# Row maximum over 67 MB: fewer, larger middle loads, more columns on GpSimd, and a first store in two halves

## The chip, the cores and the metric

The kernel runs on one core of one Trainium2 chip. The metric is device time in microseconds, the median of the runs. The profile is one more execution, taken by the hardware profiler; its span leaves out a little that the device time has (162.0 us of span beside 163.79 us for the same profiled run). "DVE" is VectorE, "PE" is TensorE, "ACT" is ScalarE, "POOL" is GpSimd, "SP" is SyncE, which here only issues loads. A trailing q (SPq, ACTq) means the engine's own queue of instructions, where DMA transfers are issued.

## The reference

The input is a float32 array of 32 x 512 x 1024. The output is the largest value of each row of 1024.

```python
def setup_inputs():
    batch, seq, dim = 32, 512, 1024
    return {"x": np.random.randn(batch, seq, dim).astype(np.float32)}

def reference(x: np.ndarray) -> np.ndarray:
    return np.max(x, axis=-1).astype(np.float32)
```

There are 16384 rows, 67.11 MB in all, and 64 KB of output. Laid over 128 partitions this is 128 rows for each partition. In this document a **block** is one row for each of the 128 partitions: 128 x 1024 values, 512 KB. There are 128 blocks to load and to reduce. A block has 1024 columns, which are 8 **column blocks** of 128.

## The kernel before

The kernel streams the blocks through a ring in SBUF that has room for 47 of them. The list `BLOCKS` says how many blocks each load carries. The loads are numbered from 0 in that order. The last two blocks come in four **pieces**, two for each, cut by column at the widths in `PIECES`.

```python
BLOCKS = [
    [2, 13, 13, 15, 14, 11, 11, 10, 8, 8, 7],
    [4, 3, 2, 2, 1, 1, 1],
]
RING = 47

SHARED = {10: (3, 6), 12: (2, 6), 14: (1, 6), 17: (1, 2)}

PIECES = [(604, 420), (568, 456)]

PLAN = """
    d0 d1 d2 d3 d4 d5 d6 d7 d8 d9 t0 d10 t1 t2 p10 d11 b0 b1 t3 d12 t4 p12 d13 b2 m10 t5 d14
    p14 d15 b3 b4 d16 m12 p17 t6 f0 b5 f1 f2 b6 m14 f3 m17
""".split()
```

`SHARED` names the loads in which GpSimd takes a part: `10: (3, 6)` means that of the last 3 blocks of load 10, six column blocks each go by another way. `PLAN` is the order of the work. Each engine takes its own steps in this order:

- `d` (direct): VectorE reduces the blocks of a load that are not shared, in one instruction.
- `t` (turn): TensorE transposes the shared column blocks into PSUM, ScalarE copies them to SBUF, GpSimd takes the maximum over the partitions.
- `b` (back): TensorE turns row 0 of GpSimd's result back into a column.
- `p` (partial): VectorE reduces the columns of a shared block that GpSimd does not take.
- `m` (merge): VectorE takes the maximum of the partial results.
- `f`: VectorE reduces a piece; the second piece of a row includes the result of the first, which lies one element ahead of it.

```python
def maximum(out, in_):
    return in_turn("DVE", nc.vector.reduce_max(out=out, in_=in_, axis=X))
# ...
def turn(k):
    j, r, q = chunks[k]
    m, parts = shared[j]
    W = q * parts * P
    ps = psum.tile([P, D], F32)
    # ... q * parts transposes on TensorE into ps
    sb = turned.tile([P, D], F32)
    in_turn("ACT", nc.scalar.copy(out=sb[:, :W], in_=ps[:, :W]))
    top = allr.tile([P, D], F32)
    in_turn("POOL", nc.gpsimd.partition_all_reduce(
        top[:, :W], sb[:, :W], P, bass_isa.ReduceOp.max))
```

A turn holds whole blocks, and at most `max(1, 8 // parts)` of them. A load is issued as soon as the steps that read its place in the ring are done (the wait is left to the semaphores); pieces follow after the last whole load.

```python
while issued < len(loads):
    start, n, src, _ = loads[issued]
    if any(readers[j] and s < start + n and start < s + k
           for j, (s, k, _, _) in enumerate(loads[:issued])):
        return
    load = nc.sync.dma_start(out=rows(issued), in_=src)
    issued += 1
# ...
while pieces:
    nc.sync.dma_start(out=pieces[0][0], in_=pieces[0][1])
    pieces.pop(0)
```

A load's place in the ring starts where the last one ended, or at 0 when it does not fit any more. Two stores end the kernel. The first carries the 112 blocks of the first list and is held until the first `f` is done, the second carries the last 16.

```python
for dst, src in views[:-1]:
    store = nc.scalar.dma_start(out=dst, in_=src)
    tc.add_manual_dep(store.ins, behind.ins.name, SYNC, reason="behind the loads")
nc.scalar.dma_start(out=views[-1][0], in_=views[-1][1])
```

Of the kernel before, what the change touches and what calls it, by code (L numbers as in the profile page):

```python
# [10 lines left out]


BLOCKS = [
    [2, 13, 13, 15, 14, 11, 11, 10, 8, 8, 7],
    [4, 3, 2, 2, 1, 1, 1],
]
RING = 47


SHARED = {10: (3, 6), 12: (2, 6), 14: (1, 6), 17: (1, 2)}  # L20

PIECES = [(604, 420), (568, 456)]

PLAN = """
    d0 d1 d2 d3 d4 d5 d6 d7 d8 d9 t0 d10 t1 t2 p10 d11 b0 b1 t3 d12 t4 p12 d13 b2 m10 t5 d14
    p14 d15 b3 b4 d16 m12 p17 t6 f0 b5 f1 f2 b6 m14 f3 m17  # L30
""".split()

NOSYNC = mybir.DependencyInfo(mybir.DependencyClass.NoSync, mybir.DependencyReason.DATA)
# [4 lines left out]
def kernel(  # L38
# [5 lines left out]
    nc = tc.nc  # L44
    P = 128
# [27 lines left out]
    def maximum(out, in_):  # L73
# [8 lines left out]
        out=colno, data0=ident, data1=ident, initial=-1.0, op0=ALU.add, op1=ALU.mult))  # L82
    in_turn("DVE", nc.vector.transpose(out=rowno, in_=colno[:, :32]))  # L83
    for q in range(1, P // 32):
        part = rowno[q * 32:(q + 1) * 32, 0:1]
        in_turn("DVE", nc.vector.tensor_scalar(  # L86
            out=part, in0=part, scalar1=float(q * 32), scalar2=None, op0=ALU.add))
    identity = in_turn("DVE", nc.vector.tensor_scalar(  # L88
        out=ident, in0=colno, scalar1=rowno[:, 0:1], scalar2=None, op0=ALU.is_equal))

    loads = []
    views = []
    last = len(PIECES)
    first = at = 0
    for sizes in BLOCKS:
        S = sum(sizes) + last * (sizes is BLOCKS[-1])
        xb = xf[first * P:(first + S) * P, :].rearrange("(p i) d -> p i d", p=P)
        dst = bass.AP(tensor=of.tensor, offset=of.offset + first * P, ap=[[S, P], [1, S]])
# [9 lines left out]
    assert first == I  # L108
    shared = [SHARED.get(j, (0, C)) for j in range(len(loads))]

# [68 lines left out]
    room = I + at * D  # L179
    for q in range(len(PIECES[0])):  # L180
        for r, widths in enumerate(PIECES):
            c, w = sum(widths[:q]), widths[q]
# [49 lines left out]
            if behind is None:  # L232
                behind = inst

    for dst, src in views[:-1]:
        store = nc.scalar.dma_start(out=dst, in_=src)
        tc.add_manual_dep(store.ins, behind.ins.name, SYNC, reason="behind the loads")
    nc.scalar.dma_start(out=views[-1][0], in_=views[-1][1])

# [28 lines left out]
```

## Time and profile before

| | |
|---|---|
| device time | 163.84 us, median of 3 runs (163.75 to 163.88) |
| span of the profiled run | 162.0 us |
| moved by the loads | 67.11 MB in 22 transfers (18 loads, 4 pieces) |
| VectorE busy | 135.5 us, 84% of the span |
| GpSimd busy | 16.2 us, of it 16.0 us in 7 reductions over the partitions |
| TensorE busy | 13.5 us; ScalarE 6.4 us |

The profile has the busy time of each engine, a picture of the span in 40 slices, the DMA queues, the chain of work that ended last, groups of instructions with busy time and the mean of one, and a timeline in order of time. A timeline row has the start, the length, the engine, the source line, the operation, what it writes and reads, the shape and how many instructions were merged into the row; the bracket at its end says how long the engine sat idle before it and what ended that. The queue numbered q1 carries the loads and q10 the stores.

### The profile page before, as it was taken

Reading aid. Unit: us, or ns where it says so; the run is one execution under the profiler, and the core shown is the slowest. Engines: PE = TensorE matmul, PEld = TensorE weight load, DVE = VectorE, ACT = ScalarE, POOL = GpSimd, SP = SyncE. Lnnn points to the kernel's source line nnn. Section 1 sums busy time; section 2 is a strip of 40 time slices with the busy share of each in tenths; the row PEclk is TensorE's granted clock in tenths of the full one; section 3 lists DMA queues with packets and bytes.
Section 4 is the critical chain, followed back from the end, with each engine's and each line's share of the span. In section 5 each row is a group of like instructions: output and inputs, shape, how many; then the busy total and the mean of one; then the engine's idle time right before and its main releaser. Section 6 shows DMA issues by size and latency. Waiting matters only on the chain.

```text
span 162.0 us, 306 instructions
## 1 busy us (share of the span) xinstructions
PE 13.5 (8%) x76; PEld 11.6 (7%) x76; DVE 135.5 (84%) x37; ACT 6.4 (4%) x8; POOL 16.2 (10%) x11
## 2 busy tenths in 40 slices
PE   0000000000000000000000000000000000746662
PEld 0000000000000000000000000000000000736541
DVE  3500079978996399989999999999999999999994
ACT  3000000000000000000000000000000000231220
POOL 0000000000000000000000000000000000197991
PEclk9999999999999999999999999999999999996555
DMA  5999999997999979999898999799999999999991
GB/s 172 508 421 421 421 421 421 473 550 303 485 485 485 396 311 425 453 405 534 356 534 356 489 400 465 344 485 388 421 485 388 424 418 453 409 431 415 407 390 37
DMA packets 3456, 67.18 MB, mean 415 GB/s; under 512 B 640, under 2 KB 896, under 8 KB 1536
## 3 DMA queue, kind: packets, MB, share of 16 engines
q1 hardware_dynamic: 3168, 67.11, 96.9%
q10 hardware_dynamic: 288, 0.07, 0.2%
HBM read 67.11 MB, written 0.07 MB: 415 GB/s over the span
## 4 chain that ended last, share of the span: by engine, by line
DVE 49%; DMA 46%; another core or an unknown queue 3%; SPq 1%; issue 0%; DVEq 0%
DVE ring L74 47%; DMA ring<-in_x_dram 46%; DVE got L74 1%; SPq L209 1%; DVEq L263 0%
## 5 line engine op out<-in xcount | busy, mean ns | idle before, releaser
L74 DVE TENSOR_REDUCE ring<-ring 128x1 f32<-128x1024 f32 (+12 forms) x21 | 131.5, 6293 | 23.3 <-DMA ring<-in_x_dram 23.1
L146 POOL PARTITION_ALL_REDUCE top<-sb x7 | 16.0, 2351 | 142.2 <-ACT sb L144 142.2
L138 PE MATMUL ps<-ident,ring 128*128 128x128 f32 x38 | 9.0, 424 | 141.3 <-DMA ring<-in_x_dram 141.0
L138 PEld LDWEIGHTS ps<-ident,ring 128*128 128x128 f32 x38 | 7.5, 224 | 141.5 <-issue 141.5
L144 ACT COPY sb<-ps 128x768 f32<-128x768 f32 (+1 forms) x7 | 5.2, 738 | 150.3 <-PE ps L138 148.9
L156 PE MATMUL got<-ident,top 1*128 1x1 f32 x38 | 4.6, 230 | 4.3 <-POOL top L146 2.9
L156 PEld LDWEIGHTS got<-ident,top 1*128 1x128 f32 x38 | 4.0, 188 | 6.0 <-POOL top L146 5.3
L74 DVE TENSOR_REDUCE got<-ring 128x3 f32<-128x768 f32 (+3 forms) x4 | 3.0, 753 | 0.0
L144 ACT ACT_TABLE_LOAD x1 | 1.3, 1283 | 0.7 <-PEq L252 0.7
L79 DVE MEMSET ident<- 128x128 f32 x1 | 0.2, 165 | 0.8 <-PEq L252 0.8
L74 DVE TENSOR_REDUCE ring<-got 128x3 f32<-128x21 f32 (+3 forms) x4 | 0.6, 160 | 0.0
L86 DVE TENSOR_SCALAR rowno<-rowno 32x1 f32<-32x1 f32 x3 | 0.4, 146 | 0.1
L81 DVE TENSOR_TENSOR_SCAN colno<-ident 128x128 f32<-128x128 f32 x1 | 0.4, 425 | 0.0
L88 DVE TENSOR_SCALAR ident<-colno,rowno 128x128 f32<-128x128 f32 x1 | 0.3, 286 | 0.0
L83 DVE STREAM_TRANSPOSE rowno<-colno 128x32 f32<-128x32 f32 x1 | 0.2, 211 | 0.0
L252 POOL MEMSET const-float32-0.0<- 128x1 f32 x1 | 0.1, 98 | 0.2 <-issue 0.2
L252 POOL MEMSET const-bfloat16-1.0<- 128x1 bf16 x1 | 0.1, 102 | 0.0
L252 POOL MEMSET const-uint8-127<- 128x1 uint8 x1 | 0.1, 101 | 0.0
L252 POOL MEMSET const-float32-1.0<- 128x1 f32 x1 | 0.1, 98 | 0.0
L80 DVE MEMSET rowno<- 128x32 f32 x1 | 0.1, 85 | 0.0
## 6 DMA issues: line engine op xcount, KB each, us to landing
ring<-in_x_dram SPq DMA_DIRECT2D x2, 6656.0 KB, 27.7
ring<-in_x_dram SPq DMA_DIRECT2D x2, 5632.0 KB, 30.9
ring<-in_x_dram SPq DMA_DIRECT2D x2, 4096.0 KB, 32.3
ring<-in_x_dram SPq DMA_DIRECT2D x1, 7680.0 KB, 53.1
ring<-in_x_dram SPq DMA_DIRECT2D x1, 7168.0 KB, 36.8
ring<-in_x_dram SPq DMA_DIRECT2D x1, 5120.0 KB, 39.2
ring<-in_x_dram SPq DMA_DIRECT2D x1, 3584.0 KB, 39.4
ring<-in_x_dram SPq DMA_DIRECT2D x3, 1024.0 KB, 38.2
```

The lines of the kernel that those rows point to most:

```text
L74: return in_turn("DVE", nc.vector.reduce_max(out=out, in_=in_, axis=X))
L79: in_turn("DVE", nc.vector.memset(ident, 1.0))
L81: in_turn("DVE", nc.vector.tensor_tensor_scan(out=colno, data0=ident, data1=ident, initial=-1.0, op0=ALU.add, op1=ALU.mult))
L83: in_turn("DVE", nc.vector.transpose(out=rowno, in_=colno[:, :32]))
L86: in_turn("DVE", nc.vector.tensor_scalar(out=part, in0=part, scalar1=float(q * 32), scalar2=None, op0=ALU.add))
L88: identity = in_turn("DVE", nc.vector.tensor_scalar(out=ident, in0=colno, scalar1=rowno[:, 0:1], scalar2=None, op0=ALU.is_equal))
L138: in_turn("PE", nc.tensor.transpose(out=ps[:, w:w + P], in_=rows(j)[:, loads[j][1] - m + r + i, c * P:(c + 1) * P], identity=ident,))
L144: in_turn("ACT", nc.scalar.copy(out=sb[:, :W], in_=ps[:, :W]))
L146: in_turn("POOL", nc.gpsimd.partition_all_reduce(top[:, :W], sb[:, :W], P, bass_isa.ReduceOp.max))
L156: in_turn("PE", nc.tensor.transpose(out=share(j)[:, c, r + i:r + i + 1], in_=tops[k][0:1, w:w + P], identity=ident[0:1, 0:1],))
L209: load = nc.sync.dma_start(out=rows(issued), in_=src)
L252: nc = _bacc.Bacc("TRN2", target_bir_lowering=False, num_devices=1)
```

## The change

The middle loads become larger and one fewer: ten numbers in the first list in place of eleven. With 17 loads and four pieces there are 21 transfers. GpSimd takes part in six loads rather than four and has 55 column blocks rather than 38 (16 + 14 + 8 + 9 + 6 + 2), in nine turns rather than seven. The pieces are cut closer to the middle. The first store, 128 partitions, is issued as two stores of 64 partitions. The aim is to take work off VectorE, to issue fewer loads, and to have the first store in smaller parts ahead of the last one.

```diff
 BLOCKS = [
-    [2, 13, 13, 15, 14, 11, 11, 10, 8, 8, 7],
+    [2, 15, 15, 15, 15, 13, 12, 10, 8, 7],
     [4, 3, 2, 2, 1, 1, 1],
 ]
 RING = 47
 
-SHARED = {10: (3, 6), 12: (2, 6), 14: (1, 6), 17: (1, 2)}
+SHARED = {8: (2, 8), 9: (2, 7), 10: (4, 2), 11: (3, 3), 13: (1, 6), 16: (1, 2)}
 
-PIECES = [(604, 420), (568, 456)]
+PIECES = [(532, 492), (520, 504)]
 
 PLAN = """
-    d0 d1 d2 d3 d4 d5 d6 d7 d8 d9 t0 d10 t1 t2 p10 d11 b0 b1 t3 d12 t4 p12 d13 b2 m10 t5 d14
-    p14 d15 b3 b4 d16 m12 p17 t6 f0 b5 f1 f2 b6 m14 f3 m17
+    d0 d1 d2 d3 d4 d5 d6 d7 t0 d8 t1 b0 d9 t2 t3 b1 t4 p9 m8 p10 b2 b3 p11 t5 t6 m9 d12 b4
+    m10 d13 t7 p13 d14 b5 b6 d15 m11 p16 t8 f0 b7 f1 f2 b8 m13 f3 m16
 """.split()
 
-    for dst, src in views[:-1]:
-        store = nc.scalar.dma_start(out=dst, in_=src)
+    half = P // 2
+    for p in (0, half):
+        store = nc.scalar.dma_start(out=views[0][0][p:p + half], in_=views[0][1][p:p + half])
         tc.add_manual_dep(store.ins, behind.ins.name, SYNC, reason="behind the loads")
     nc.scalar.dma_start(out=views[-1][0], in_=views[-1][1])
```

## The prediction

> **What bounds the kernel now.** I began with the page's picture of the span and its queue table, because the change touches loads and engines alike.
>
> ```profile
> DVE  3500079978996399989999999999999999999994
> ...
> DMA  5999999997999979999898999799999999999991
> ...
> q1 hardware_dynamic: 3168, 67.11, 96.9%
> ```
>
> Both look bound: VectorE has no gap in the last 22 slices, and the load queue's packets fill 96.9% of 16 engines' span. So the second view is the timeline of VectorE, where a bracket shows who ends each wait.
>
> ```profile
> 21.27 14.02 DVE L74 TENSOR_REDUCE ring<-ring 128x13 f32<-128x13312 f32 x1 [13.45 <-DMA ring<-in_x_dram]
> 37.02 14.02 DVE L74 TENSOR_REDUCE ring<-ring 128x13 f32<-128x13312 f32 x1 [1.72 <-DMA ring<-in_x_dram]
> 55.16 16.15 DVE L74 TENSOR_REDUCE ring<-ring 128x15 f32<-128x15360 f32 x1 [4.12 <-DMA ring<-in_x_dram]
> 72.10 71.24 DVE L74 TENSOR_REDUCE ring<-ring 128x14 f32<-128x14336 f32 x7 [0.79 <-DMA ring<-in_x_dram]
> ...
> 157.12 1.95 DVE L74 TENSOR_REDUCE ring<-ring 128x1 f32<-128x604 f32 x3
> 158.99 0.15 DVE L74 TENSOR_REDUCE ring<-got 128x1 f32<-128x7 f32 x1
> 159.06 0.62 DVE L74 TENSOR_REDUCE ring<-ring 128x1 f32<-128x457 f32 x1
> 159.59 0.15 DVE L74 TENSOR_REDUCE ring<-got 128x1 f32<-128x3 f32 x1
> ```
>
> The first four rows start within 0.02 us of a landing, so their distances are distances of landings: 15.75 us for 13 blocks, 18.14 for 15, 16.94 for 14. That is 1.21 us per block, 433 GB/s, with no hole. The third view, busy time by windows, says whether that rate holds to the end. The last two columns are the DMA share and GB/s.
>
> ```profile
> 80.00:100.00 20.00, 0.00 (x0) 0.00 (x0) 20.00 (x3) 0.00 (x0) 0.00 (x0) 1.00 0.99 426
> 100.00:120.00 20.00, 0.00 (x0) 0.00 (x0) 19.88 (x2) 0.00 (x0) 0.00 (x0) 1.00 0.99 426
> 140.00:150.00 10.00, 6.36 (x37) 5.84 (x37) 10.00 (x5) 3.14 (x4) 7.47 (x3) 0.84 0.99 417
> 156.00:158.00 2.00, 0.99 (x5) 0.62 (x6) 2.00 (x5) 0.37 (x1) 2.00 (x2) 0.50 1.05 383
> 158.00:159.00 1.00, 0.75 (x7) 0.66 (x6) 1.00 (x3) 0.00 (x0) 0.67 (x1) 0.50 0.35 116
> ```
>
> It does, save for a loss among the small loads at the end. From issue plus time to landing, the trace has the last whole load (17) landing at 156.23, and the four pieces at 157.06, 157.80, 158.35 and 158.92. VectorE starts load 17's partial at 156.25, 0.02 after its landing, and runs back to back from there: three pieces from 157.12, a merge, the last piece at 159.06, a merge ending at 159.745. So both are true at once: the loads run without a hole from 1.7 to 158.5, and VectorE is exactly even with them when they stop. Behind that lies a fixed end:
>
> ```profile
> 157.93 0.38 ACTq L236 DMA_DIRECT2D out_dram<-ring  x1
> 159.78 0.34 ACTq L238 DMA_DIRECT2D out_dram<-ring  x1
> ```
>
> The last store is issued 0.03 after the last merge, lands 1.41 later (161.19), and the closing semaphores bring the span to 162.02: 2.28 us from the merge's end.
>
> [...] 13 blocks alone take 14.02 us and 15 take 16.15, 1.067 us a block or 1.042 ns an element[...]. Back to back an instruction starts some 0.08 before the one ahead ends, so it costs 1.067 n + 0.06 us for n blocks[...].
>
> **The change part by part.**
>
> *Loads.* Landing distances fit 1.205 n + 0.075 us for a load of n blocks: 8 blocks took 9.72, one took 1.28, 15 took 18.14. The 112 blocks of the first list stay 112. One load fewer takes one 0.075 off. The second list is unchanged, and the four pieces have the same bytes (2.69 us together, assumed equal). Last landing: 158.92 - 0.075 = 158.85.
>
> *The ring, which could undo that.* With sizes 2, 15, 15, 15 the ring of 47 is exactly full, and each later load waits for the VectorE steps that read its place. Landings by the fit: load 1 at 23.7, then 41.8, 60.0, 78.1, 93.9, 108.4, 120.5, 130.2, and load 9 at 138.7. VectorE ends d1 at 39.9, d2 at 58.0, d3 at 76.1, d4 at 94.3, d5 at 108.2, d6 at 121.4. So load 4 is issued at 39.9 while the queue has work until 60.0; load 5 at 58.0 (work until 78.1), load 6 at 76.1 (93.9), load 7 at 94.3 (108.4), loads 8 and 9 at 108.2 (120.5), loads 10 and on at 121.4 (138.7). The least reserve is 12 us. The trace also shows that a piece is issued just as the load eight transfers ahead lands (piece 0 at 138.83, load 10 at 138.81); after, piece 0 follows load 9 at 138.7 and piece 3 follows load 12 near 149.8, 9 us before its data come. No hole.
>
> *VectorE.* 17 column blocks more go to GpSimd: 17 x 128 x 1.042 ns = 2.27 us less work. Where does it go? Load 8 loses 2 blocks, load 10 loses one, loads 9 and 11 gain half and three eighths. VectorE lags load 7's landing by 0.8 us and load 8's by 1.8 (d8 from 132.0 to 138.6), then meets load 9 (138.7): d9 starts at 138.8 on a landing, with some 0.2 us of waiting. From there, back to back: d9 5.40, p9 0.34, merge 0.08, p10 3.27, p11 2.07, merge 0.08, d12 2.20, merge 0.08 make 152.3, even with load 13 (152.3). Then d13, p13, d14, d15 and a merge, 3.8 us, end near 156.15, as load 16 lands (156.16). So the saving becomes waiting and slack ahead of 139; at the end VectorE is even with the loads again.
>
> *The end.* From p16's start to the last merge VectorE has 768 + 532 + 520 + 493 + 505 = 2818 elements; before they were 768 + 604 + 568 + 421 + 457 = 2818. Same number, same instructions: 159.745 - 156.252 = 3.49 us. Start 156.17, end 159.67, against 159.745. The last piece reaches VectorE at 158.92 by this count, its data at 158.85: even again. Being 48 elements wider than before, it could cost 0.05 if data were the limit.
>
> *GpSimd.* By the rows of its reductions, 768 columns take 2.50 to 2.58 us and 256 take 1.13; linear between and beyond, 2.83 ns a column: 3.3 us for 1024, 2.94 for 896, 1.5 for 384. Nine turns (1024, 1024, 896, 896, 1024, 768, 384, 768, 256) make 23 us against 16.0. From landing to GpSimd's start a turn took 2.5 us (138.81 to 141.35). Load 8's two turns run 133.2 to 139.8; load 9's 141.4 to 147.0; then 1024 to 150.3, 768 to 152.8, 384 to 154.2. The turn of load 13 can start at 155.04, as load 14's did before. The merges that need these come at 144.5, 149.9, 152.2 and 156.1, TensorE's way back taking up to 0.85 us: slack 2, 2, 0.8 and 0.9 us. The last two turns are those of before, with 0.5 us slack.
>
> *Stores.* The first store is issued after the first piece at 157.79, in two steps of up to 0.38 us, done by 158.55; the last is due at 159.70. Its packets follow the last load packets (158.47 before), as before. Nothing on the path; no gain either.
>
> *Sum.* -0.075 us. 163.84 becomes 163.77; I say 163.76.
>
> **The rivals.**
>
> 1. VectorE is the bound, and 2.27 us less work is 2.27 us less time: about 161.6. For it: no idle from 72 on, and 47% of the chain is its rows. Against it: the last load lands at 158.92 whatever VectorE does, and 3.1 us of end follow. Without that landing's moving, at most the 0.1 us from landing to the last piece's start could be won.
> 2. A late GpSimd holds a merge, and VectorE, in order, stands behind it. The middle turns form one chain from 141.4 to 154.2 with 0.8 us slack at load 10's merge. If turns were 10% slower than the line through two sizes, the merges of loads 10 and 11 would start some 0.5 to 1 us late: 164.2 to 164.7. The 2.50 to 2.58 measured at one size speak against it.
> 3. The ring, now exactly full with larger loads, starves the queue. A 1 us hole would be 1 us of time. The 12 us reserve speaks against it.
> 4. Store packets earlier in time get ahead of the last load packets, each way 0.1 to 0.2 us. Before, 0.3 us lay between the two queues' packets.
>
> **Range and chances.** Rivals 2 and 4 give a tail of up to 0.9 us on the slow side, each with a chance below one in ten; on the fast side the tail can't yield over some 0.2. Repeated runs differ by 0.13. So 163.76, and 163.4 to 164.1 eight times in ten. 2% is 3.3 us, which only a large hole in the loads or a broken chain of turns would give: faster 0.01, same 0.98, slower 0.01.
>
> **What would show it.** Right: last landing near 158.85, load packets without a hole, VectorE idle some 0.2 to 0.4 us on landings between 93 and 139, p16 starting on load 16's landing, GpSimd busy near 23 us in nine reductions, the last merge ending near 159.67. Wrong: VectorE waiting on TensorE before a merge (rival 2), 20 us windows below 415 GB/s between 20 and 140 (rival 3), the last piece's landing later than 158.95 with stores in front (rival 4), or a span under 161.5, which would mean that the load time is not what sets the end.

## The result, and the profile after

The changed kernel takes 165.28 us (165.05 to 165.33, 6 runs) against 163.84 us. The ratio is 1.0085, with a 95% interval of 1.0072 to 1.0098. It is slower by 1.44 us where the prediction had 0.08 us faster, and it lies outside the predicted range. The two times lie within 2% of each other, as the prediction's chances had it, but the difference is wrong in size and in sign. The execution that was profiled took 165.05 us, the shortest of the six. Its span is 163.17 us against 162.02 before, so the profile shows 1.15 us of the loss.

The timeline of VectorE in the changed kernel, from its wait for load 4 on:

```profile
78.18 30.08 DVE L74 TENSOR_REDUCE ring<-ring 128x15 f32<-128x15360 f32 x2 [1.99 <-DMA ring<-in_x_dram]
108.44 30.14 DVE L74 TENSOR_REDUCE ring<-ring 128x12 f32<-128x12288 f32 x3 [0.19 <-DMA ring<-in_x_dram]
138.81 5.49 DVE L74 TENSOR_REDUCE ring<-ring 128x5 f32<-128x5120 f32 x1 [0.23 <-DMA ring<-in_x_dram]
...
156.29 0.96 DVE L74 TENSOR_REDUCE got<-ring 128x1 f32<-128x768 f32 x1
157.16 0.70 DVE L74 TENSOR_REDUCE ring<-ring 128x1 f32<-128x532 f32 x1
158.78 1.37 DVE L74 TENSOR_REDUCE ring<-ring 128x1 f32<-128x520 f32 x2 [0.92 <-DMA ring<-in_x_dram]
160.07 0.15 DVE L74 TENSOR_REDUCE ring<-got 128x1 f32<-128x7 f32 x1
160.14 0.67 DVE L74 TENSOR_REDUCE ring<-ring 128x1 f32<-128x505 f32 x1
160.73 0.15 DVE L74 TENSOR_REDUCE ring<-got 128x1 f32<-128x3 f32 x1
```

Up to the row at 157.16 this is the predicted kernel to about 0.1 us. Then VectorE waits 0.92 us for the second piece, a wait that the kernel before does not have. By issue and time to landing, the four pieces land at 156.94, 158.75, 159.39 and 160.04. Before they landed at 157.06, 157.80, 158.35 and 158.92. The first piece is on time, and the second and all behind it are about 1 us late.

The DMA queues of the changed kernel name something new:

```profile
q1 hardware_dynamic: 3024, 67.11, 96.2%
q10 hardware_dynamic: 304, 0.07, 0.2%
q8 instruction: 1, 0.02, 0.0%
```

The columns are packets, MB and share of 16 engines. One packet of the kind "instruction" went over queue 8; the trace record has it at 156.392 with 16384 bytes and 1.095 us. The profile before has no such packet in its span. The windows of the changed kernel show what it did to the loads (last two columns: DMA share, GB/s):

```profile
157.00:158.00 1.00, 0.47 (x5) 0.47 (x5) 0.85 (x2) 0.37 (x1) 0.93 (x2) 0.50 1.01 369
158.00:158.50 0.50, 0.32 (x4) 0.24 (x3) 0.00 (x0) 0.00 (x0) 0.50 (x1) 0.50 0.39 137
158.50:159.00 0.50, 0.34 (x2) 0.28 (x2) 0.23 (x1) 0.00 (x0) 0.11 (x1) 0.50 0.06 24
```

From 158.5 to 159.0 the share is 0.06, one sixteenth, at 24 GB/s (433 / 16 is 27). I read this as one DMA engine alone, which still works off its part of the pieces while fifteen are done. The packet records agree. In the last microsecond before the instruction packet 16.9 load packets are under way on average (neighbouring records overlap a little, so it can be more than 16), while it runs 15.8, just behind it 16.8. And from 158.4 to 159.59 the load packets run in single file, some 0.08 us each. So in this trace one late engine is enough to make three landings late, by 0.95, 1.04 and 1.12 us against the kernel before.

That gave theory A: TensorE's program has grown from 76 to 110 pairs of weight load and matmul (a pair for each transpose, two transposes for each column block), it now needs one more fetch of instructions, and the packet of that fetch holds one DMA engine for 1.1 us among the last loads. Rival B was the store in two halves, whose packets could get between the pieces; against it, the first packet of a store comes at 159.08, when the second piece has already landed late. Rival C was the pieces' new widths.

### The profile page after: what moved, and what is told of

The parts are those of the page before. It is cut to its first block, busy times and chain, and to the rows that moved or that the text cites. A ratio compares the mean times of both kernels' runs of the same rounds, so it can differ in the third digit from the quotient of the medians.

```text
span 163.2 us, 385 instructions
## 1 busy us (share of the span) xinstructions
PE 18.9 (12%) x110; PEld 16.3 (10%) x110; DVE 133.6 (82%) x37; ACT 8.5 (5%) x10; POOL 23.0 (14%) x13
## 4 chain that ended last, share of the span: by engine, by line
DMA 67%; DVE 29%; another core or an unknown queue 1%; SPq 0%; issue 0%; DVEq 0%
DMA ring<-in_x_dram 67%; DVE ring L74 29%; SPq L209 0%; DVEq L264 0%
## 5 line engine op out<-in xcount | busy, mean ns | idle before, releaser
L74 DVE TENSOR_REDUCE ring<-ring 128x15 f32<-128x15360 f32 (+11 forms) x18 | 125.0, 6963 | 26.3 <-DMA ring<-in_x_dram 26.3
L146 POOL PARTITION_ALL_REDUCE top<-sb x9 | 22.8, 2577 | 135.4 <-ACT sb L144 135.3
L138 PE MATMUL ps<-ident,ring 128*128 128x128 f32 x55 | 12.3, 403 | 134.2 <-DMA ring<-in_x_dram 134.2
L138 PEld LDWEIGHTS ps<-ident,ring 128*128 128x128 f32 x55 | 10.2, 212 | 134.4 <-issue 133.5
L144 ACT COPY sb<-ps 128x1024 f32<-128x1024 f32 (+4 forms) x9 | 7.2, 811 | 148.2 <-PE ps L138 148.2
L156 PE MATMUL got<-ident,top 1*128 1x1 f32 x55 | 6.8, 236 | 6.0 <-POOL top L146 5.9
L74 DVE TENSOR_REDUCE got<-ring 128x2 f32<-128x256 f32 (+4 forms) x5 | 7.2, 1459 | 0.1
L156 PEld LDWEIGHTS got<-ident,top 1*128 1x128 f32 x55 | 6.1, 200 | 8.3 <-POOL top L146 7.6
L74 DVE TENSOR_REDUCE ring<-got 128x2 f32<-128x16 f32 (+4 forms) x6 | 1.0, 159 | 0.0
```

What stands on the lines that cost most here:

```text
L138: in_turn("PE", nc.tensor.transpose(out=ps[:, w:w + P], in_=rows(j)[:, loads[j][1] - m + r + i, c * P:(c + 1) * P], identity=ident,))
L146: in_turn("POOL", nc.gpsimd.partition_all_reduce(top[:, :W], sb[:, :W], P, bass_isa.ReduceOp.max))
L156: in_turn("PE", nc.tensor.transpose(out=share(j)[:, c, r + i:r + i + 1], in_=tops[k][0:1, w:w + P], identity=ident[0:1, 0:1],))
```

## The experiments

Each was timed beside the kernel before on the same chip; that kernel's medians were 163.74 to 163.82 us in the three groups, and every ratio is to the one of its group.

**1. The changed kernel without 16 ways back.**

```diff
-    d0 d1 d2 d3 d4 d5 d6 d7 t0 d8 t1 b0 d9 t2 t3 b1 t4 p9 m8 p10 b2 b3 p11 t5 t6 m9 d12 b4
+    d0 d1 d2 d3 d4 d5 d6 d7 t0 d8 t1 d9 t2 t3 t4 p9 m8 p10 b2 b3 p11 t5 t6 m9 d12 b4
 # ...
     def merge(j):
         _, n, _, col = loads[j]
+        if j == 8:
+            in_turn("DVE", nc.vector.memset(res[:, col + n - shared[j][0]:col + n], 0.0))
+            return
```

> The changed kernel without the 16 ways back of load 8 on TensorE; the two columns of its result are filled with zeros instead of the merge, so those two blocks of the output are left out. Everything else, stores and pieces too, is as in the changed kernel. Theory A (TensorE's longer program needs one more fetch of instructions, a 16 KB packet on queue 8, that holds one DMA engine for 1.1 us among the last loads): no packet on queue 8, the last piece lands near 158.9 instead of 160.04, time 163.7 to 163.95. Rival B (the first store in two halves gets between the last pieces): unchanged, 165.1 to 165.3. Rival C (the new widths of the pieces are slower to load): unchanged, 165.1 to 165.3.

Measured: 164.11 us, ratio 1.0019 (1.0011 to 1.0028). Stores and piece widths are those of the changed kernel, yet the last piece lands at 158.90. Rivals B and C fall as the main cause. But theory A missed too: it expected no packet on queue 8 and at most 163.95 us. The packet is still there, later, at 158.30, when the loads are all but over (their last packet ends at 158.38). 0.31 us of loss remain. This is the timeline of ScalarE's queue in experiment 1, with the two half stores in one row:

```profile
157.81 1.99 ACTq L240 DMA_DIRECT2D out_dram<-ring  x2
159.89 0.54 ACTq L242 DMA_DIRECT2D out_dram<-ring  x1
```

The changed kernel takes 1.19 us for the same two issues and 0.35 for the last. The second half is issued at 158.37, while the packet runs, and that issue alone takes 1.43 us. It landed at 161.09 and the last store at 161.50, 1.61 us after its issue where the changed kernel has 1.43. That the fetch causes this, too, fits in time but was not tested.

**2. The kernel before with 36 idle transposes more.**

```diff
+    PAD = 36
+    while PAD:
+        ps = psum.tile([P, D], F32)
+        for w in range(min(PAD, D // P)):
+            in_turn("PE", nc.tensor.transpose(out=ps[:, w * P:(w + 1) * P], in_=ident, identity=ident))
+        PAD -= min(PAD, D // P)
+
     loads = []
```

> The kernel before with 36 more transposes of the identity on TensorE at the start, into PSUM that nothing reads; TensorE then has 112 pairs of weight load and matmul, 110 in the changed kernel, and no other engine has anything new. Theory A: one 16 KB packet on queue 8 between 155 and 158, pieces landing about 1.1 us late, time 164.7 to 165.4. Rivals B and C: 163.75 to 163.95, as the kernel before.

Measured: 163.83 us, ratio 1.0011 (0.9995 to 1.0027). The time that theory A expected was missed. The packet appears as expected, with nothing but TensorE changed, but it starts at 158.73, after the loads' last packet (its end is at 158.47). There it costs nothing in the end: the first store lands at 160.99 in place of 159.52, still ahead of the last store's 161.20. One of the 12 runs took 165.32; it has no profile. So with more pairs alone (112, 76 before) a fetch comes; when its packet starts is not simply when TensorE reaches a certain pair: at that time 100 of 110 pairs are done in the changed kernel, 92 of 94 in experiment 1. TensorE's granted clock in this experiment is 0.55 of full speed, 0.95 in the kernel before, so a lower clock of TensorE is not what costs time.

**3 and 4. The stores alone.** Experiment 3 is the kernel before with the first store in two halves, experiment 4 the changed kernel with one store; each is the store's part of the diff, applied or undone.

```diff
-    for dst, src in views[:-1]:
-        store = nc.scalar.dma_start(out=dst, in_=src)
+    half = P // 2
+    for p in (0, half):
+        store = nc.scalar.dma_start(out=views[0][0][p:p + half], in_=views[0][1][p:p + half])
```

> The kernel before with the first store in two halves of 64 partitions, nothing else. Theory A: 163.75 to 163.95. Rival B: 1 us or more slower, 164.8 to 165.3. Rival C: 163.75 to 163.95.

> The changed kernel with the first store in one piece again. Theory A: the fetch stays, 165.0 to 165.4. Rival B: 163.7 to 164.0. Rival C: 165.0 to 165.4.

Measured: 163.82 us, ratio 1.0002 (0.9993 to 1.0011), for the halves in the kernel before, and 165.25 us, ratio 1.0089 (1.0074 to 1.0104), for the whole store in the changed one, with the packet on queue 8 at 156.33. The split has no part in the loss that can be seen, and it brings nothing. Rival B is out.

**5. The changed kernel without 30 ways back**, the edit of experiment 1 for loads 8 and 9 (`if j in (8, 9)`, and b0 to b3 out of the plan). Four blocks of the output are left out.

> The changed kernel without the 30 ways back of loads 8 and 9 on TensorE (four blocks of the output are left out, their columns filled with zeros in place of two merges). TensorE then has 80 pairs of weight load and matmul[...]. Theory A (the fetch is the whole loss): no packet on queue 8 at all, last piece at 158.85 to 158.95, 163.70 to 163.90. Rival (only part of the loss is the fetch; the rest is in pieces, stores or VectorE): above 164.0 without any packet on queue 8.

Measured: 163.78 us, ratio 1.0001 (0.9993 to 1.0010). Its DMA queues have two lines, and no third:

```profile
q1 hardware_dynamic: 3024, 67.11, 96.9%
q10 hardware_dynamic: 304, 0.07, 0.2%
```

The end of its VectorE timeline has no wait between the first piece and the last:

```profile
157.14 1.97 DVE L74 TENSOR_REDUCE ring<-ring 128x1 f32<-128x532 f32 x3
159.03 0.15 DVE L74 TENSOR_REDUCE ring<-got 128x1 f32<-128x7 f32 x1
159.10 0.67 DVE L74 TENSOR_REDUCE ring<-ring 128x1 f32<-128x505 f32 x1
159.69 0.15 DVE L74 TENSOR_REDUCE ring<-got 128x1 f32<-128x3 f32 x1
```

Loads, pieces, stores, turns and GpSimd's reductions are the changed kernel's. TensorE's program is shorter by 60 instructions, VectorE has two fills of 0.06 us in place of two merges of 0.16, and the whole loss is gone. Rival C is out: the pieces with the new widths take 2.73 us from load 16's landing (156.25 to 158.98), against 2.69 before.

**6 and 7. The kernel before with 60 and with 110 idle transposes** (the edit of experiment 2 with another number), to move the fetch and see whether a held engine catches up. The border of which their expectations speak is the number of pairs from which on a fetch comes. It lies above 76 (the kernel before, no packet on queue 8) and at or below 94 (experiment 1, one packet).

> The kernel before with 60 transposes of the identity on TensorE at the start. The border is then passed with the ways back near 146, and the fetch should run between 146 and 153, among loads. Theory A1 (each of the 16 engines has a fixed share of every load and no speed in reserve, so the held one stays late to the end): all landings after it, the last piece too, about 1.1 us late, 164.8 to 165.3. A2 (the held engine catches up in the rest of the loads): 163.8 to 164.2. Rival (number of TensorE's instructions doesn't matter): 163.75 to 163.95, no packet on queue 8 among the loads.

> The kernel before with 110 transposes of the identity at the start. The border is passed inside them, near 20 us, and the fetch should run among the loads 1 to 3, with 110 us of loads behind it and VectorE waiting for loads anyway. A1: the held engine stays 1.1 us late to the last piece, 164.8 to 165.3. A2: 163.75 to 164.0. A packet on queue 8 before 60 is expected by both.

Measured: 165.04 us, ratio 1.0076 (1.0061 to 1.0091), and 165.13 us, ratio 1.0082 (1.0066 to 1.0099). Neither kernel differs from the one before in anything but idle work at the start, so the loss is reproduced. In experiment 6 the place was missed (the packet starts at 155.82, not between 146 and 153), the size was not: the last piece lands at 160.27 in place of 158.92. Its VectorE timeline has the new wait, here for the first piece:

```profile
158.47 1.95 DVE L74 TENSOR_REDUCE ring<-ring 128x1 f32<-128x604 f32 x3 [1.36 <-DMA ring<-in_x_dram]
```

Experiment 7 decides between A1 and A2. Its TensorE timeline and, below, a window of its DMA queues from 18 to 20 us show the idle work and the packet:

```profile
2.57 14.65 PE L95 MATMUL ps<-ident 128*128 128x128 f32 x110 [2.57 <-DVE ident L88]
```

```profile
q1 hardware_dynamic: 16, 0.85, 99.9%
q8 instruction: 1, 0.02, 3.0%
```

The packet starts at 18.74 and lasts 0.98 us. The packet records show the place that it takes. Load packets of 53248 bytes come in rounds of 16 there, and each takes 1.97 us. In the round that starts from 18.51 to 18.88 only 15 load packets start, and the instruction packet stands in the place of the sixteenth. That load packet follows at 19.70 and takes 2.46 us, so its engine is done with it at 22.16, where 18.74 + 1.97 = 20.70 would have been its time: 1.46 us late. VectorE's first wait of a middle load in experiment 7, and its windows at the end:

```profile
22.63 14.02 DVE L74 TENSOR_REDUCE ring<-ring 128x13 f32<-128x13312 f32 x1 [14.85 <-DMA ring<-in_x_dram]
```

```profile
158.50:159.00 0.50, 0.01 (x1) 0.01 (x1) 0.50 (x2) 0.28 (x1) 0.50 (x2) 0.50 0.07 25
159.00:159.50 0.50, 0.50 (x5) 0.50 (x6) 0.50 (x2) 0.00 (x0) 0.50 (x1) 0.50 0.07 25
```

Load 1 ends VectorE's wait at 22.63 in place of 21.27, 1.36 us late. Load 10 lands at 140.15 in place of 138.81, and the last piece at 160.21 in place of 158.92, 1.29 us late. At the end one engine again works alone, at 25 GB/s. The engine that was held at 19 us has caught up with next to nothing (1.36 to 1.29) in 140 us of loads. A1 holds: with all 16 busy (a DMA share of 0.98 to 1.03 in the 20 us windows of the kernel before from 20 to 140), what was taken from one of them at 19 us is still missing at the end, as is what was taken at 156.

**8. The new loads with the old share of GpSimd.**

```diff
-SHARED = {8: (2, 8), 9: (2, 7), 10: (4, 2), 11: (3, 3), 13: (1, 6), 16: (1, 2)}
+SHARED = {9: (3, 6), 11: (2, 6), 13: (1, 6), 16: (1, 2)}
```

The plan is that of before, with the numbers of 17 loads.

> The changed kernel's loads, pieces and stores with GpSimd's share of before (38 column blocks in four loads, 76 pairs on TensorE). Theory A: no packet on queue 8 and last piece at 158.9; but VectorE has 2.27 us more to do, less the 0.23 us it waits for load 9, so the last merge ends near 161.5 and the time is 165.4 to 165.9. Rival (larger loads cost nothing by themselves): 163.7 to 164.0.

Measured: 165.47 us, ratio 1.0101 (1.0086 to 1.0116). There is no packet on queue 8, and the last piece lands at 158.89, but VectorE is late:

```profile
108.41 36.60 DVE L74 TENSOR_REDUCE ring<-ring 128x12 f32<-128x12288 f32 x4 [0.19 <-DMA ring<-in_x_dram]
144.92 0.95 DVE L74 TENSOR_REDUCE got<-ring 128x3 f32<-128x768 f32 x1
...
160.61 0.67 DVE L74 TENSOR_REDUCE ring<-ring 128x1 f32<-128x505 f32 x1
161.19 0.15 DVE L74 TENSOR_REDUCE ring<-got 128x1 f32<-128x3 f32 x1
```

It does not wait after 108.41, and starts the last piece 1.7 us after its landing. So the larger middle loads need the larger share of GpSimd: with them VectorE waits longer early on (25.1 us for loads in all, 23.1 before), and what it then lacks in time must go elsewhere.

**9. The new share with the old loads**, pieces and store, and a plan to match.

```diff
-SHARED = {10: (3, 6), 12: (2, 6), 14: (1, 6), 17: (1, 2)}
+SHARED = {9: (2, 8), 10: (2, 7), 11: (4, 2), 12: (3, 3), 14: (1, 6), 17: (1, 2)}
```

> The kernel before with the new share of GpSimd alone: 55 column blocks in the six loads that carry the same numbers of blocks from the end (9, 10, 11, 12, 14, 17), the old load sizes, pieces and single store. TensorE has 110 pairs again. Theory A: one packet on queue 8 near 156, last piece near 160, 165.0 to 165.4, although VectorE has 2.27 us less to do than before and no load has changed. Rival (VectorE's relief shows once the loads are not enlarged): 163.5 to 163.8.

Measured: 165.25 us, ratio 1.0084 (1.0067 to 1.0101), with the packet on queue 8 at 156.32. The timeline of VectorE in experiment 9:

```profile
138.85 5.49 DVE L74 TENSOR_REDUCE ring<-ring 128x5 f32<-128x5120 f32 x1 [1.96 <-DMA ring<-in_x_dram]
...
158.54 1.93 DVE L74 TENSOR_REDUCE ring<-ring 128x1 f32<-128x604 f32 x3 [1.27 <-DMA ring<-in_x_dram]
```

VectorE's relief turns into 1.96 us of waiting at load 10, and the share alone is enough for the whole loss of the changed kernel (1.43 us here).

## Why the prediction was wrong

- **Loads and ring: right.** Landings of loads 1 to 9 were predicted at 23.7, 41.8, 60.0, 78.1, 93.9, 108.4, 120.5, 130.2 and 138.7; they came at 23.7, 41.9, 60.0, 78.2, 93.9, 108.4, 120.6, 130.3 and 138.8. No hole from the ring, so rival 3 of the prediction falls. The 124 blocks from load 0's landing to that of the last whole load, 65.01 MB, came at 431.6 GB/s, and at 431.3 before. That no list of loads could raise this rate was not shown.
- **VectorE: right.** d9 starts on a landing after 0.23 us of waiting, as predicted, and p16 at 156.29, 0.09 after load 16's landing (156.17 predicted). Its relief brought no time, which also answers rival 1; experiment 9 shows the relief as waiting.
- **GpSimd: right.** Nine reductions, 22.8 us busy (23 predicted, though the sizes given for the turns add up to 23.5), and no merge waited for them. Rival 2 falls.
- **Stores: harmless as predicted**, though a half costs 0.54 to 0.61 us to issue rather than at most 0.38. Rival 4 falls by experiments 3 and 4. It had the right shape, foreign packets among the last loads, but named the wrong queue and, as an estimate, 0.1 to 0.2 us.
- **The step that failed** is in the part on loads: "the four pieces have the same bytes (2.69 us together, assumed equal)", and with it "Last landing: 158.92 - 0.075 = 158.85". The pieces took 3.84 us from load 16's landing (156.20 to 160.04). The bytes were the same, but one DMA engine was taken out for 1.1 us in the middle of them. The prediction took loads and stores for everything that these engines carry, and counted TensorE's further work only as the delay of a way back (up to 0.85 us), where its 34 further pairs held up no step of VectorE: past its start, VectorE waits for loads alone in the profile, 26.3 us in all. The packet of kind "instruction" went over the same DMA engines (in experiment 7 it stands in the place of a sixteenth load packet), and with 110 pairs one such packet, 16384 bytes, falls into the span.
- **The sum then closes.** In the profiles the last landing moved by 160.04 - 158.92 = 1.12 us, the end of the last merge by 160.88 - 159.745 = 1.13, the span by 1.15. In the other profiles with such a packet among the loads (experiments 4, 6, 7 and 9) the last piece is 1.17 to 1.35 us late, so the delay differs from run to run. Take the longer program away and the changed kernel runs as predicted: 163.78 in experiment 5 against 163.76.
- **The 0.075 us of one load fewer** can't be seen: experiment 5's ratio of 1.0001 has an interval wider than the 0.05% it would be. From load 0's landing to that of the last whole load the profiles have 150.63 us in the changed kernel and 150.72 before, but kernels with the same 18 loads already spread from 150.65 to 150.72.

Three things stay open. The border is known only in part: kernels with 76 and 80 pairs have no fetch in the span, kernels with 94, 110, 112, 136 and 186 have one. What sets the packet's start is not settled: in experiment 7 it starts 1.5 us after the last idle transpose has ended (18.74 and 17.22), in experiment 2 only after the last load packet (158.73 and 158.47). And the last piece is up to 1.35 us late where the packet's own record is 1.0 to 1.1: experiment 7 shows 0.5 us more in the load packet just behind it, but not why that one is slower, nor whether it is so among the pieces.

No version beat the kernel before. Larger middle loads need more columns on GpSimd (experiment 8: 1.7 us without), more columns cost four TensorE instructions for each column block, and those bring the fetch (experiment 9: 1.43 us).

## What to carry to other kernels

When a kernel keeps every DMA engine busy to its end, ask what else uses these engines. Here the instruction stream did: TensorE was busy for 12% of the span, and yet its longer program was not free, with one packet of 16384 bytes and the last piece 1.12 us late. Look for a line of the kind "instruction" among the DMA queues, and for a last window in which the DMA share is one sixteenth (0.06 here). And when two resources finish even, ask what the relieved one will wait for. Loads and VectorE did here, and taking work off VectorE only made it wait (1.96 us at load 10 in experiment 9); what the change added elsewhere was then all that showed in the time (1.43 us).

## What was not expected of the hardware

That a fetch of instructions shows in the time was not expected: the prediction has no item for it. One packet of 16384 bytes cost 1.1 us of one DMA engine (1.095 in the changed kernel, 0.98 in experiment 7), and 1.3 to 1.4 us of a kernel that loads without a pause (experiments 6, 7 and 9). It was fully hidden only in experiment 2, where the packet came at 158.73, after the loads' last packet (158.47).

That a delay of one of 16 DMA engines at 19 us is still nearly whole at 160 us was not expected either: 1.36 us at load 1 and 1.29 at the last piece.
